# A two-layer generator block on one core: early loads for C and D, bias tables, first modulation in four column groups, first sums by token rows

## The chip, the cores and the metric

The kernel runs on one core of one Trainium2 chip. The metric is the device time of one execution in microseconds (us). A core has TensorE (PE: matrix products; PEld is its weight load), VectorE (DVE), ScalarE (ACT), GpSimd (POOL) and SyncE (SP), which here issues nearly all DMAs; sixteen DMA engines move the data. SBUF and PSUM are the core's two on-chip memories, and PSUM takes what TensorE writes.

## What is computed

There are 256 context tokens and 1024 latent tokens of width 1024, and two layers. Each layer normalises and modulates its input, multiplies it by one wide projection (3600 columns), gives slices of the result to four head groups A to D, and adds the output projection and an MLP of hidden width 4096. Group A is a gated linear recurrence, B a matrix memory; C is attention of every query to all keys, D attention to a window of 8 rows by 16 columns plus the context, with a learned bias by row and column distance (`rpb`). The modulation is a product of two vectors, silu(c) and silu(c_ctx), with `w_mod` (1024 by 6144 in each layer).

```python
def _layer(x, xc, c, c_ctx, w_mod, b_mod, g1, g2, w_in, lb, hgrn_g, mlstm_b, mlstm_g,
           qn_g, kn_g, rpb, w_out, w1, w2, rope, need_ctx):
    mod = jnp.split((jax.nn.silu(c) @ w_mod + b_mod)[:, None, :], 6, axis=-1)
    modc = jnp.split((jax.nn.silu(c_ctx) @ w_mod + b_mod)[None, None, :], 6, axis=-1)
    zl = _split_in(_modulate(_rmsnorm(x, g1), mod[0], mod[1]) @ w_in)
    zc = _split_in(_modulate(_rmsnorm(xc, g1), modc[0], modc[1]) @ w_in)
    ...
    a_c, a_l = _bidir_prefix(_hgrn2_scan, ...)
    ...
    b_c, b_l = _bidir_prefix(_mlstm_scan, ...)
    ...
    c_l = _merge(_gqa_latent(_apply_rope(ql, *rope), _apply_rope(kl, *rope), vl, kc_, vc_))
    d_l = _merge(_neighbourhood_attn(nq, nk, nv, ck, cv, rpb))
    y = jnp.concatenate([a_l, b_l, c_l, d_l], axis=-1) @ w_out
    x = x + mod[2] * y
    x = x + mod[5] * _sqrelu_mlp(_modulate(_rmsnorm(x, g2), mod[3], mod[4]), w1, w2)
    ...

def reference(...):
    for l in range(DEPTH):
        x, xc = _layer(...)
    return _rmsnorm(x, final_norm_g)
```

## The kernel before

**Tiling.** Tokens are cut into ten tiles of 128, and these into three blocks `TBS` of 256 (the context), 512 and 512. A float32 product is taken as three matmuls of two-part operands (`mm3`, L380 to L382: hi by hi, lo by hi, hi by lo). For each weight chunk a DMA brings `raw`, POOL makes the high part (L136) and DVE the low part (L145). `job` runs a projection over a list of token tiles (kind T, tokens on the partitions) or blocks (kind F, features on the partitions).

**Order.** The code is written as stages, and a scheduler reorders each engine's instructions by the program's order and its own estimate of times; an engine then runs its list in order, and SP's list of DMAs is such a list. SBUF places come from pools, and a pool opened on a place that another has left waits for the last reader of what was there.

**Stages.** `build` runs `start` for each block (x or ctx rows are loaded as `xt`, transposed on TensorE, squared by feature rows and summed), with `modulation_pe` for the chunks of 512 columns 0, 2, 1, 3 of `w_mod`, and `norm`. `modulation_pe` multiplies with two weight columns, so an accumulation of 8 matmuls fills 2 partitions of `pm`. Then `mixing(l)` runs `project_a`, in layer 0 with chunks 4 to 11 of the modulation in between (`more`; on DVE, L249, from the `mw` ring), then `a_forward`, which reads A's inputs back from DRAM (`zA`, `zL`; L731 to L739), `project_b`, `project_c` and `project_d`, the B recurrence (`b_forward`, its products at L1037, `b_backward`), and the attention. `finish` (L668) ends a head output of A or B: transposes (L683), a copy to `ofe` on ACT (L685), and a store to `oT` issued by SP (L686).

**The bias.** `bias_pad` and `bias_rows` write each bias row 64 times, padded to 127 columns, to DRAM (`rp`); `group_d` reads it back with a skewed access pattern (`braw`) and POOL multiplies by a column mask and adds another (L1232, L1233) into `BE`. `BI` is a copy of `BE` for the inner rows.

**The attention.** `attention` opens its pools, loads `KTc`, `VSc` (C's keys and values), `KTd`, `Vd` (D's), and queries `QTc`, `QTd` tile by tile, two buffers each. The order of steps is three of C, then D and C by turns. A step's scores go to the PSUM tile `S` (L1182 for C, L1265 for D); DVE takes a maximum (L1133, L1137), ACT the exponential (L1138), and TensorE transposes (L1159) and multiplies by the values (L1203, L1296). In the first four steps `S` has one buffer, since the recurrence still holds the others; later it has three.

## Time and profile before

| what | value |
|---|---|
| time, median of 3 runs | 3778.57 us (3771.67 to 3780.75) |
| the profiled execution's own time | 3784.66 us |
| its span, first to last instruction | 3782.9 us |
| TensorE, VectorE busy | 97%, 59% of the span |
| ScalarE, GpSimd busy | 29%, 31% of the span |
| mean granted TensorE clock | 0.968 of full speed |

The rows below come from a profile of one execution. A row of the timeline gives start and duration in us, the engine, the line, the operation, the tiles written and read, the shape, how many of a kind, and in brackets the engine's idle time just before, with what ended it. A row of busy times gives a stretch, its length, the busy us of PE, PEld, DVE, ACT and POOL with the number of instructions, then TensorE's granted clock, the busy share of the DMA engines and the GB/s they moved. A row of a group by line gives a count, busy us and mean ns, and behind the second bar the idle time before it; with one line asked for, it gives ns as least, median and most, and the first and last start.

### The profile page before, as it was taken

How to read it: one execution, taken by the hardware profiler on the slowest of the kernel's cores; microseconds unless marked ns; L12 is line 12 of the kernel's file. 1: busy time of each engine (PE TensorE's matmuls, PEld its weight loads, DVE VectorE, ACT ScalarE, POOL GpSimd, SP SyncE). 2: the span in 40 equal slices, each digit the busy share in tenths (PEclk: the TensorE clock that was granted, in tenths of full speed). 3: DMA queues.
4: the chain of work that ended last, by engine and by line, in shares of the span. 5: the costliest groups of instructions: out<-in, count | busy, mean ns of one | idle time of the engine just before them, and what ended most of it. 6: DMA issues, size and time to landing. Idle time of an engine off the chain costs nothing. (4 is left out here: it accounts for less than half of the span.)

```text
span 3782.9 us, 60590 instructions
## 1 busy us (share of the span) xinstructions
PE 3654.4 (97%) x22276; PEld 3080.5 (81%) x22276; DVE 2237.0 (59%) x5368; ACT 1107.9 (29%) x2847; POOL 1155.0 (31%) x1645
## 2 busy tenths in 40 slices
...
GB/s 238 232 195 98 94 89 120 210 131 94 120 39 62 70 76 78 65 81 78 61 48 95 123 146 89 101 101 195 115 78 34 124 42 50 52 45 51 50 45 65
DMA packets 374991, 366.61 MB, mean 97 GB/s; under 512 B 63334, under 2 KB 333350, under 8 KB 372902
## 3 DMA queue, kind: packets, MB, share of 16 engines
...
## 5 line engine op out<-in xcount | busy, mean ns | idle before, releaser
L380 PE MATMUL mm<-hi,whi 128*128 128x512 f32 (+1 forms) x1948 | 721.5, 371 | 4.7 <-POOL hi L136 4.7
L381 PE MATMUL mm<-lo,whi 128*128 128x512 f32 (+1 forms) x1948 | 720.9, 370 | 2.9 <-DVE lo L145 2.9
L382 PE MATMUL mm<-hi,wlo 128*128 128x512 f32 (+1 forms) x1948 | 723.1, 371 | 0.0
L136 POOL TENSOR_SCALAR whi<-raw 128x512 fp32r<-128x512 f32 x392 | 268.7, 686 | 1126.5 <-PE mm L381 840.2
L1397 DVE SCALAR_TENSOR_TENSOR x<-mm,mod,x 128x512 f32<-128x512 f32 (+1 forms) x648 | 431.6, 686 | 195.8 <-PE mm L382 192.1
L145 DVE TENSOR_TENSOR wlo<-raw,whi 128x512 fp32r<-128x512 f32 x392 | 312.2, 798 | 311.9 <-POOL whi L136 306.7
L1381 ACT ACTIVATE r<-mm 128x512 f32<-128x512 f32 (+1 forms) x162 | 89.0, 550 | 1331.3 <-PE mm L382 1331.1
L382 PE MATMUL mm<-hh,wlo 128*128 128x512 f32 (+1 forms) x1252 | 463.1, 371 | 0.0
L381 PE MATMUL mm<-hl,whi 128*128 128x512 f32 (+1 forms) x1252 | 461.2, 370 | 1.4 <-DVE hl L145 1.4
L380 PE MATMUL mm<-hh,whi 128*128 128x512 f32 (+1 forms) x1252 | 450.2, 371 | 3.5 <-POOL hh L136 3.4
L380 PE MATMUL mm<-whi,hi 128*128 128x256 f32 (+1 forms) x1496 | 432.6, 290 | 6.5 <-POOL hi L136 3.1
L381 PE MATMUL mm<-wlo,hi 128*128 128x256 f32 (+1 forms) x1496 | 429.2, 288 | 1.2 <-DVE wlo L145 1.2
L382 PE MATMUL mm<-whi,lo 128*128 128x256 f32 (+1 forms) x1496 | 425.2, 288 | 5.2 <-DVE lo L145 5.2
L380 PEld LDWEIGHTS mm<-hi,whi 128*128 128x128 f32 x1948 | 370.0, 190 | 68.8 <-POOL hi L136 5.0
L381 PEld LDWEIGHTS mm<-lo,whi 128*128 128x128 f32 x1948 | 368.6, 189 | 67.6 <-DVE lo L145 5.3
L382 PEld LDWEIGHTS mm<-hi,wlo 128*128 128x128 f32 x1948 | 368.3, 189 | 62.7 <-issue 0.5
L380 PEld LDWEIGHTS mm<-whi,hi 128*128 128x128 f32 x1496 | 287.5, 192 | 13.0 <-POOL hi L136 4.0
L382 PEld LDWEIGHTS mm<-whi,lo 128*128 128x128 f32 x1496 | 286.0, 193 | 10.1 <-DVE lo L145 6.4
L381 PEld LDWEIGHTS mm<-wlo,hi 128*128 128x128 f32 x1496 | 287.7, 192 | 5.0 <-DVE wlo L145 1.4
L145 DVE TENSOR_TENSOR hl<-r,hh 128x512 fp32r<-128x512 f32 (+1 forms) x162 | 114.7, 708 | 294.5 <-POOL hh L136 294.5
L381 PEld LDWEIGHTS mm<-hl,whi 128*128 128x128 f32 x1252 | 236.9, 189 | 45.1 <-DVE hl L145 2.2
L380 PEld LDWEIGHTS mm<-hh,whi 128*128 128x128 f32 x1252 | 235.3, 190 | 45.7 <-POOL hh L136 4.6
...
## 6 DMA issues: line engine op xcount, KB each, us to landing
raw<-in_w_mlp SPq DMA_DIRECT2D x256, 256.0 KB
raw<-in_w_in SPq DMA_DIRECT2D x112, 256.0 KB
...
```

The source lines that it names most:

```text
L136: self.nc.gpsimd.tensor_scalar(out, in_, 1.0, 0.0, op0=ALU.mult, op1=ALU.add)
L145: self.nc.vector.tensor_tensor(lo, src, hi.bitcast(F32), op=ALU.subtract)
L380: self.nc.tensor.matmul(ps, lhsT=lh, rhs=rh, start=(k == 0), stop=False)
L381: self.nc.tensor.matmul(ps, lhsT=lh, rhs=rl, start=False, stop=False)
L382: self.nc.tensor.matmul(ps, lhsT=ll, rhs=rh, start=False, stop=(k == n - 1))
L1381: nc.scalar.activation(r[:, 0:n], ps[:, 0:n], AF.Relu)
L1397: nc.vector.scalar_tensor_tensor(xk, ps[:, 0:n], self.mod[l][:, 40 + mt, v:v + 1], xk, op0=ALU.mult, op1=ALU.add)
```

## The change

1. The bias rows in DRAM go (8 DMAs from DRAM to DRAM, half of them in layer 0's MLP). In `more` of layer 0, four calls of `bias_tables` each load two column masks for 16 query columns, broadcast to 120 rows (2 layers, 4 heads, 15 row distances), multiply and add on POOL with a skewed view of the bias rows, and store a finished table `btab`. They take three buffers of the `mw` ring. `BE` is then one load for each head and half of the partitions; the two POOL passes over `braw` go.
2. The first modulation is one accumulation: two weight columns padded to 32, and output chunk g in partitions 32g to 32g+31 of one PSUM tile. Loads are 128 rows by 1024 columns, 16 of them; the result is copied once and transposed four times. The `mw` ring has 6 buffers instead of 4 there.
3. The first sums of squares are taken by ACT from the `xt` rows (Square with an accumulated output), not from the transposed x by ACT, DVE, POOL and a matmul with ones.
4. Loads of x come behind those of `w_mod`, and those of small rows behind x; ctx and the modulation have high priority. The first two jobs of `project_a` alternate by token tiles.
5. The attention's pools and first loads are opened before `b_backward`, in the places that the activations of the projections leave. `qC` in DRAM is stored by token tile, so that a row of a `QTc` load is 2 KB instead of 512 bytes. `project_d` takes its v and q jobs by turns, block by block, with both weights loaded ahead.
6. `finish` issues its store to `oT` from ACT instead of SP (36 stores).

```diff
-    def bias_rows(self, l, part):
-
-        with self.tc.issue_after(self.last_w):
-            self.nc.sync.dma_start(out=self.rps[l].rearrange("h d q c -> (h d) q c")[:, 16 * part:16 * part + 16, :],
-                                   in_=self.rpad[60 * l:60 * l + 60, :].unsqueeze(1).broadcast_to([60, 16, 127]))
...
+    def bias_tables(self, P, part):
+
+        nc, a = self.nc, self.a
+        if part == 0:
+            self.brow = self.t(P, [120, 127], tag="rs", bufs=1)
+            nc.gpsimd.memset(self.brow, 0.0)
+            nc.sync.dma_start(out=self.brow[:, 48:79], in_=a["na_rpb"].rearrange("l h d c -> (l h d) c"))
+            self.btab = self.dp.tile([120, 64, 64], F32, name="btab", tag="btab")
+        va, bg, m = [self.t(P, [128, 2, 512], tag="mw", bufs=self.mwb)[0:120].rearrange("p c (q j) -> p (c q) j", j=64) for _ in range(3)]
+        q0 = 16 * part
+        for i, z in enumerate((va, bg)):
+            nc.sync.dma_start(out=z, in_=a["k_col"][q0:q0 + 16, i * 64:i * 64 + 64].unsqueeze(0).broadcast_to([120, 16, 64]))
+        r = self.brow[:, 0:1]
+        diag = bass.AP(tensor=r.tensor, offset=r.offset + 63 - q0, ap=[r.ap[0], [-1, 16], [1, 64]])
+        nc.gpsimd.tensor_tensor(m, diag, va, op=ALU.mult)
+        nc.gpsimd.tensor_tensor(m, m, bg, op=ALU.add)
+        nc.sync.dma_start(out=self.btab[:, q0:q0 + 16, :], in_=m)
...
+        lh = self.t(mp, [128, NK, 32], tag="lhp", bufs=1)
+        nc.gpsimd.memset(lh, 0.0)
+        nc.vector.tensor_copy(lh[:, :, 0:2], self.lhC)
         rows = self.t(pm, [128, 512], tag="pm")
-        for _, _, u, src in self.raw_wide(mp)(self.a["w_mod"][l], ch):
-            for i in range(2):
-                k = u + i
-                nc.tensor.matmul(rows[0:2, :], lhsT=self.lhC[:, k, :], rhs=src[:, i, :], start=(k == 0), stop=(k == NK - 1))
-        r = self.t(mp, [2, 512], tag="mr", bufs=1)
-        nc.vector.tensor_copy(r, rows[0:2, :])
+        for k in range(NK):
+            for c in range(2):
+                t = self.t(mp, [128, 2, 512], tag="mw", bufs=self.mwb)
+                ins = nc.sync.dma_start(out=t.rearrange("p c n -> p (c n)"), in_=self.a["w_mod"][l][k * 128:(k + 1) * 128, c * 1024:c * 1024 + 1024])
+                self.last_mod = ins.ins
+                for i in range(2):
+                    g = c * 2 + i
+                    nc.tensor.matmul(rows[g * 32:g * 32 + 32, :], lhsT=lh[:, k, :], rhs=t[:, i, :], start=(k == 0), stop=(k == NK - 1))
+        r = self.t(mp, [128, 512], tag="mr", bufs=1)
+        nc.vector.tensor_copy(r, rows)
         pt = self.t(pm, [128, 512], tag="pm")
         for m in range(4):
-            nc.tensor.transpose(pt[:, m * 2:m * 2 + 2], r[:, m * 128:m * 128 + 128], self.ident[0:2, 0:2])
-        bb = self.bmod[l][:, ch * 4:ch * 4 + 4].unsqueeze(2).broadcast_to([128, 4, 2])
-        nc.vector.tensor_tensor(self.mod[l][:, ch * 4:ch * 4 + 4, :], pt[:, 0:8].rearrange("p (m v) -> p m v", v=2), bb, op=ALU.add)
+            nc.tensor.transpose(pt[:, m * 128:m * 128 + 128], r[:, m * 128:m * 128 + 128], self.ident)
...
+        if l == 0 and which == 0:
+            ps = self.t(np_, [128, 4], tag="sqs", bufs=2)
+            nc.vector.tensor_tensor(ps[:, 0:nb], self.sqt[tb][:, 0:nb, 0], self.sqt[tb][:, 0:nb, 1], op=ALU.add)
...
-        self.qC = d("qC", [128, 4, 1280])
+        self.qC = d("qC", [NT, 128, 4, 128])
...
-        self.job(l, h, "T", 768, 256, al[:6], f0, w0)
-        self.job(l, h, "T", 256, 256, al[:6], val, w1)
+        for ts in (al[:2], al[2:6]):
+            self.job(l, h, "T", 768, 256, ts, f0, w0)
+            self.job(l, h, "T", 256, 256, ts, val, w1)
...
-        self.job(l, h, "T", 3344, 256, list(range(NT)), d_v)
-        self.job(l, h, "F", 2832, 256, [1, 2] if last else [0, 1, 2], feat(self.qD, 0.125))
...
+        w = self.a["w_in"][l]
+        wv = self.wchunk(w, 0, NK, 3344, 256)
+        wq = self.wchunk(w, 0, NK, 2832, 256, sg)
+        fq = feat(self.qD, 0.125)
+        for tb, (t0, n) in enumerate(TBS):
+            self.job(l, h, "T", 3344, 256, list(range(t0 // 128, (t0 + n) // 128)), d_v, wv)
+            if tb or not last:
+                self.job(l, h, "F", 2832, 256, [tb], fq, wq)
...
-            nc.sync.dma_start(out=self.oT[tb][:, kt:kt + 2, off:off + 128], in_=s)
+            nc.scalar.dma_start(out=self.oT[tb][:, kt:kt + 2, off:off + 128], in_=s)
...
+        t0 = NCTX if last else 0
+        qt, ots = {t: self.q_load(Q, self.qC[t], "QTc") for t in (t0, t0 + 1)}, {}
...
-                    base = self.rps[l][h, 1 - par + 7 * i:8 - par + 7 * i, :, :]
-                    src = bass.AP(tensor=base.tensor, offset=base.offset + 63, ap=[[126, 64], [64 * 127, 7], [1, 64]])
-                    nc.sync.dma_start(out=raw[par * 64:par * 64 + 64, :, :], in_=src)
-                nc.gpsimd.tensor_tensor(raw, raw, col[:, 0, :].unsqueeze(1).broadcast_to([128, 7, 64]), op=ALU.mult)
-                nc.gpsimd.tensor_tensor(BE[:, h, 7 * i:7 * i + 7, :], raw, col[:, 1, :].unsqueeze(1).broadcast_to([128, 7, 64]), op=ALU.add)
...
+            for par in range(2):
+                r0 = 60 * l + 15 * h + 1 - par
+                nc.sync.dma_start(out=BE[par * 64:par * 64 + 64, h, :, :], in_=self.btab[r0:r0 + 14, :, :].rearrange("d q j -> q d j"))
...
+        pools = ExitStack()
+        D_, K_, Q_, B_, C_ = [pools.enter_context(self.pool(n, side=side)) for n in ("gd", "gkv", "gq", "gdb", "gc")]
...
+        c = self.group_c(l, K_, C_, Q_, PS)
+        d = self.group_d(l, K_, D_, PS, B_, D_BI)
...
+            self.last_x = nc.sync.dma_start(out=xt, in_=src).ins
+            for q in range(2):
+                sq = self.t(np_, [128, 512], tag="sq", bufs=2)
+                nc.scalar.activation(sq, xt[:, q * 512:q * 512 + 512], AF.Square, accum_out=self.sqt[tb][:, off // 128, q:q + 1])
...
-        for k in range(NK):
-            self.square(np_, tb, k, xs[tb][:, k, :])
...
-                    if l == 0 and i == 3:
-                        self.bias_pad(mp)
                     for ch in ([4], [5], [6, 7], [8, 9], [10, 11], [])[i]:
                         if l == 0:
                             self.modulation(0, ch, mp, True, self.raw_wide(mp), ("ma0", "ma1"), 2)
+                    if l == 0 and i < 4:
+                        self.bias_tables(mp, i)
...
+        att, close_att = self.attention(l, Y)
         close_gx()
         self.gx, close_gx = self.open(f"gy{l}", space=PSUM, side="right")
         with self.pool(f"gbb{l}", side=X) as bb:
             self.b_backward(l, bb, tail)
         close_gb()
         close_tail()
-        self.attention(l, Y)
+        att()
+        close_att()
...
-            self.rawb, self.mwb = 2, 4
+            self.rawb, self.mwb = 2, 6
...
-                    self.start(xs, ld, np_, 0)
-                    for ch in (0, 2, 1, 3):
-                        self.modulation_pe(0, ch, mp, pm)
+                    with tc.high_priority(offset=2000):
+                        self.start(xs, ld, np_, 0)
+                        self.modulation_pe(0, mp, pm)
                     h[0] = self.norm(0, 0, 0, xs[0], acts[0][0], np_)
-                    self.setup_rows()
-                    self.lower_bound(mp)
-                    self.start(xs, ld, np_, 1)
+                    with tc.issue_after(self.last_mod):
+                        self.start(xs, ld, np_, 1)
                     h[1] = self.norm(0, 0, 1, xs[1], acts[1][0], np_)
-                    self.start(xs, ld, np_, 2)
+                    with tc.issue_after(self.last_mod):
+                        self.start(xs, ld, np_, 2)
+                    with tc.issue_after(self.last_x):
+                        self.setup_rows()
+                        self.lower_bound(mp)
                     close_ld()
                     acts.append(self.open("act2", side=Y))
```

**Order of instructions, start of the program, TensorE.** `mm` at L1458 (L1476 after) are transposes of x, `pm` is the modulation, `nn<-dg` a part of the norm, and L380 (L393 after) the first projection. Before:

```order
L340 MATMUL nn_299<-dg_296,ones 128x256
L1458 MATMUL mm_389<-ident,xt_387 128x128 x4
L268 MATMUL pm_208<-mw_213,lhC 2x512 x2
L1458 MATMUL mm_514<-ident,xt_512 128x128 x4
L268 MATMUL pm_208<-mw_217,lhC 2x512 x2
L1458 MATMUL mm_562<-ident,xt_554 128x128 x4
L340 MATMUL nn_466<-dg_461,ones 128x512
L273 MATMUL pm_227<-ident,mr_225 128x2 x4
L268 MATMUL pm_233<-mw_234,lhC 2x512 x2
L380 MATMUL mm_785<-whi_738,hi_56_303 128x256
L381 MATMUL mm_785<-wlo_739,hi_56_303 128x256
```

After:

```order
L278 MATMUL pm_172<-mw_177,lhp_169 32x512 x2
L353 MATMUL nn_261<-dg_258,ones 128x256
L278 MATMUL pm_172<-mw_181,lhp_169 32x512 x2
L278 MATMUL pm_172<-mw_233,lhp_169 32x512 x2
L283 MATMUL pm_239<-ident,mr_237 128x128 x4
L1476 MATMUL mm_314<-ident,xt_308 128x128 x4
...
L1476 MATMUL mm_498<-ident,xt_492 128x128 x4
L353 MATMUL nn_391<-dg_386,ones 128x512
L1476 MATMUL mm_504<-ident,xt_492 128x128 x4
L393 MATMUL mm_729<-whi_682,hi_45_265 128x256
L394 MATMUL mm_729<-wlo_683,hi_45_265 128x256
```

All modulation matmuls now stand ahead of all transposes of latent x, and the first projection matmul stands behind all of both; before, the three were mixed.

**Order of DMAs ahead of a_forward, SP.** `z`, `v`, `Lh` and `Ll` are A's inputs, `raw` weights of the projections. Before:

```order
L216 DMA rp_2208<-rpad 60x16x127
L731 DMA z_3037<-zA_0_658 128x768
L733 DMA v_3039<-zA_0_658 128x256
L739 DMA Lh_3041<-zL_0_668 64x2x256 x2
L739 DMA Ll_3042<-zL_0_668 64x2x256 x2
L364 DMA raw_5559<-in_w_in 128x2x256
L216 DMA rp_2208<-rpad 60x16x127
L739 DMA Lh_3307<-zL_0_670 64x2x256 x2
```

After:

```order
L377 DMA raw_5330<-in_w_in 128x2x256
L490 DMA zB_0_641<-sg_2941 128x256
L377 DMA raw_5342<-in_w_in 128x2x256
L746 DMA z_3010<-zA_0_602 128x768
L748 DMA v_3012<-zA_0_602 128x256
L754 DMA Lh_3014<-zL_0_612 64x2x256 x2
L754 DMA Ll_3015<-zL_0_612 64x2x256 x2
L754 DMA Lh_3081<-zL_0_613 64x2x256 x2
```

The `rp` copies are gone from ahead of the reads of A's inputs.

**Order of instructions at the start of layer 1's attention, TensorE.** `mx`, `bx` belong to the B recurrence (L1037, or L1052 after, stands once or twice in each of its steps); `S` are scores of C. Before:

```order
L990 MATMUL mx_27910<-SB_4906_27093,qk_27751 128x130
L1068 MATMUL bx_28022<-ve_27859,Pm_28002 128x65 x4
L869 MATMUL mx_27941<-SA_4264_23688,bst_27937 128x128
L683 MATMUL mx_27945<-ident,fsq_27844 128x128 x2
L1057 MATMUL bx_28072<-MM_27089,pick_27091 128x512
L1058 MATMUL bx_28072<-ml_27085,identr 128x512
L1027 MATMUL mx_27971<-ident,qk_27965 128x128 x2
L1182 MATMUL S_29246<-KTc_29177,QTc_29238 128x512
```

After:

```order
L698 MATMUL mx_27563<-ident,fsq_27462 128x128 x2
L1042 MATMUL mx_27589<-ident,qk_27583 128x128 x2
L1052 MATMUL mx_27598<-wv_27594,kT_27592 64x130 x2
L1083 MATMUL bx_27640<-ve_27477,Pm_27620 128x65 x4
L1062 MATMUL bx_27716<-qk_27690 128x128 x2
L1005 MATMUL mx_27635<-SB_4900_27032,qk_27476 128x130
L884 MATMUL mx_27666<-SA_4258_23627,bst_27662 128x128
L1198 MATMUL S_29162<-KTc_28771,QTc_28775 128x512
L1062 MATMUL bx_27720<-qk_27690 128x128 x2
L1072 MATMUL bx_27724<-MM_27028,pick_27030 128x512
```

Before, the first scores stand ahead of the last of the five recurrence steps that are left behind the last projection matmul; after, they stand behind the second of five.

## Rows read from the trace of the kernel before

**Rows 1.** busy time of the engines, from the page

```profile
PE 3654.4 (97%) x22276; PEld 3080.5 (81%) x22276; DVE 2237.0 (59%) x5368; ACT 1107.9 (29%) x2847; POOL 1155.0 (31%) x1645
```

**Rows 2.** busy time by stretch, columns as told above: four stretches

```profile
0.00:100.00 100.00, 79.86 (x402) 48.80 (x403) 58.59 (x114) 46.97 (x88) 38.18 (x47) 0.95 0.65 229
100.00:260.00 160.00, 159.39 (x1327) 159.24 (x1325) 128.53 (x213) 32.16 (x70) 43.78 (x52) 0.98 0.73 225
700.00:820.00 120.00, 101.72 (x587) 75.41 (x586) 91.89 (x276) 61.30 (x202) 69.50 (x89) 0.80 0.71 199
2600.00:2780.00 180.00, 145.38 (x756) 106.78 (x754) 128.58 (x389) 75.99 (x247) 87.09 (x112) 0.70 0.50 148
```

**Rows 3.** TensorE's timeline at the start of the program

```profile
52.18 0.28 PE L381 MATMUL mm<-wlo,hi 128*128 128x256 f32 x1
52.30 0.28 PE L380 MATMUL mm<-whi,hi 128*128 128x256 f32 x1
58.92 8.72 PE L268 MATMUL pm<-mw,lhC 128*2 128x512 f32 x16
```

**Rows 4.** the DMA queue's timeline at the start, and a stretch of busy times

```profile
7.79 2.27 SPq L281 DMA_DIRECT2D mw<-in_w_mod  x3
39.55 16.05 SPq L281 DMA_DIRECT2D mw<-in_w_mod  x6
...
30.00:40.00 10.00, 8.72 (x52) 5.10 (x51) 5.77 (x9) 8.03 (x15) 4.80 (x5) 1.00 1.05 391
```

**Rows 5.** groups of instructions by line, 0 to 100 us

```profile
L380 PE MATMUL mm<-whi,hi 128*128 128x256 f32 x66 | 19.5, 308 | 4.1 <-POOL hi L136 2.6 <-ACT F L495 1.4
L145 DVE TENSOR_TENSOR lo<-u,hi 128x512 fp32r<-128x512 f32 x13 | 11.1, 865 | 2.4 <-POOL hi L136 2.3
```

**Rows 6.** the stop before a_forward: TensorE, DMA queue, busy times

```profile
279.79 0.55 PE L748 MATMUL mx<-Lh,sx 128*128 128x256 f32 x1 [7.44 <-DMA Lh<-zL]
...
268.44 0.96 SPq L216 DMA_DIRECT2D rp<-rpad  x1
270.57 2.57 SPq L739 DMA_DIRECT2D Lh<-zL  x2
...
272.00:280.00 8.00, 0.56 (x4) 0.37 (x4) 0.00 (x0) 0.00 (x0) 0.00 (x0) 0.84 1.06 186
```

**Rows 7.** TensorE's timeline in the attention, two column groups

```profile
803.14 0.66 PE L1203 MATMUL op<-ptc,VSc 128*64 128x128 f32 x8 [0.16 <-ACT ptc L1200]
```

**Rows 8.** instructions of the bias and of the modulation, by line

```profile
L1232 POOL TENSOR_TENSOR braw<-braw,col x16: 1126/1136/1313, 723.8 to 2731.7; 128x448 f32<-128x448 f32 x16
...
L249 DVE SCALAR_TENSOR_TENSOR ma<-mw,lhC,ma x112: 735/742/1231, 110.7 to 256.8; 128x512 f32<-128x512 f32 x112
```

**Rows 9.** layer 0's attention: TensorE, busy times

```profile
709.15 0.39 PE L382 MATMUL mm<-hi,wlo 128*128 128x512 f32 x1
730.15 0.58 PE L1182 MATMUL S<-KTc,QTc 128*128 128x256 f32 x1
750.38 0.56 PE L1182 MATMUL S<-KTc,QTc 128*128 128x256 f32 x1
...
709.00:770.00 61.00, 54.22 (x276) 41.92 (x274) 37.82 (x113) 27.17 (x96) 27.15 (x33) 0.69 0.90 262
770.00:880.00 110.00, 98.21 (x818) 73.61 (x819) 104.46 (x380) 79.08 (x250) 79.46 (x118) 0.95 0.40 110
```

**Rows 10.** layer 1's attention: TensorE, busy times

```profile
2610.74 0.39 PE L382 MATMUL mm<-hi,wlo 128*128 128x512 f32 x1
2658.78 0.78 PE L1182 MATMUL S<-KTc,QTc 128*128 128x512 f32 x1
2672.44 0.73 PE L1182 MATMUL S<-KTc,QTc 128*128 128x512 f32 x2 [2.22 <-ACT Pc L1138]
...
2610.00:2660.00 50.00, 46.83 (x204) 36.17 (x202) 30.94 (x88) 22.05 (x80) 16.98 (x21) 0.59 0.85 279
```

**Rows 11.** the head output's store, by line

```profile
L686 SPq DMA_DIRECT2D oT<-ofe x36: 359/377/1030, 648.0 to 2760.9; - x36
```

115 lines of the change are left out of this document (48 added, 67 removed).

## The prediction

> **What bounds the kernel now.** The first view to read is the page's busy time: TensorE is busy for 97% of the span, every other engine for 59% or less [rows 1]. A change can gain only where TensorE stands idle or runs at less than its full clock, so the second view is the busy time by stretch. Idle time plus busy time times the missing clock is what a stretch loses. The first 100 us lose 20.1 + 79.9 x 0.05 = 24 us; 700 to 820 us, where layer 0's attention begins, lose 18.3 + 101.7 x 0.20 = 39 us; 2600 to 2780 us, the same place in layer 1, lose 34.6 + 145.4 x 0.30 = 78 us, and there TensorE is at 0.70 of the clock [rows 2]. The change works on these three stretches and on a fourth, a stop of 7.44 us at 272 us [rows 6]. Each has its own limit, read there. Work that TensorE keeps elsewhere is left as it is, so the sum is made of four terms.
>
> **The start.** The loads of the first modulation set the pace: they begin at 7.79 us, and the last six wait in SP's list from 39.55 to 55.60 us behind x and buffers [rows 4]. Projection matmuls begin at 52 us, but stop again for the modulation, which takes 8.72 us at 58.92 us alone [rows 3]. How late the flow is can be counted. Two matmuls of 256 columns start 0.12 us apart (52.18 and 52.30) [rows 3]; up to 100 us there are 66 triples, 198 matmuls [rows 5], so 23.8 us of work: the same as a flow without gaps from 76.2 us on.
> After the change, 16 loads of 0.524 MB come first behind ctx (1.05 MB), then x (4.19 MB). The queue moves 391 GB/s when full [rows 4]: ctx is in at 10.5 us, the modulation at 32, x at 42.7. TensorE must keep up. Eight modulation matmuls take 8.72 us, 1.09 us each [rows 3]; two after one another would take 2.18 us a load, against 1.34 us of DMA. But they go to different column groups. In the attention four matmuls of 128 columns in two groups (eight records, with their weight loads) take 0.66 us [rows 7], where the same columns one after another would cost 1.09 us: so a pair costs some 2.18 x 0.66 / 1.09 = 1.32 us, and DMA stays the limit.
> The Trainium skill speaks both for and against this pairing ("TensorE: Matmul & The Clock Gate", Part 3): it gives 2.38 times for three column tiles of 512 columns, but says that a weight load overlaps a running matmul only in another row group, and column tiles share theirs. By the first the sum stays at its 70 us; by the second a pair costs up to the 2.18 us of two in turn, and the sum would be 57 us, as in rival (a). The row of the attention holds such weight loads too, and it stands with the first.
> The first projection matmul stands behind the last x transposes, at about 44 us. The context block gives 96 matmuls, 11.5 us, then the larger blocks must be normalised: 16 low parts of 0.865 us on DVE [rows 5], and a like pass before each, beside the low parts of weights. I expect 8 us of waiting there: a flow as if begun at 52 us. **Gain 76.2 - 52 = 24, of which I take 23 us.** It is 31 without that wait, and 8 if DVE's passes hold the larger blocks for twice as long and the modulation ends late too. The sums of squares that leave DVE and POOL and the squares that move to `xt` rows on ACT cost nothing more: the ACT passes run beside loads.
>
> **The stop before a_forward.** TensorE waits 7.44 us for A's inputs; SP issued a 476 KB `rp` copy at 268.44 us, just ahead of the reads at 270.57 us, and all DMA engines are then full at 186 GB/s [rows 6]. The copies are gone from that place. A read of 0.5 MB still has to land. **Gain 6 us**, from 0 (the reads wait for the stores of their own data) to 10 (the slower clock behind the stop goes too).
>
> **Layer 0's attention.** The last projection matmul is at 709.15 us, the first scores at 730.15, the second only at 750.38 us; the DMA engines are 90% busy between, with keys, values and queries [rows 9]. Those loads now stand earlier in SP's list, with C's queries in rows of 2 KB. But behind it DVE is the limit: busy for 104.5 of 110 us from 770 us on [rows 9]. What DVE has to do is unchanged, so the gain is at most its idle time before that, 61 - 37.8 = 23 us [rows 9]. **Gain 15 us**, two thirds of that cap, since the B recurrence that fills the stretch is a chain of its own; from 5 to 22.
>
> **Layer 1's attention.** From the last projection matmul (2610.74 us) to the first scores (2658.78 us) it takes 48 us, at 0.59 of the clock with the DMA engines 85% busy [rows 10]. In TensorE's list the first scores now stand behind two of the five recurrence steps left there, not behind four. At equal steps that is 2/5 of 48 = 19 us after the last projection: 29 us earlier. I take 3 off, as mixed steps slow each other. **Gain 26 us.** The upper end is DVE's idle time from 2600 to 2780 us, 180 - 128.6 = 51 us [rows 2], less 6 for what a chain never fills: 45. The lower end is 10, when scores and steps only change places.
>
> **The other edits.** Bias tables: four parts each move three times 0.49 MB in pieces of 256 bytes, 5.9 MB. The nearest row is the `rp` copy in pieces of 508 bytes: 186 GB/s at a full queue [rows 6], so 32 us of all DMA engines, between 100 and 260 us, where they are busy for 73% and 43 us are left [rows 2]. On POOL, eight passes over 1024 elements at 1.136 us for 448 [rows 8] are 21 us, beside 43.8 us of 160 [rows 2]; 32 passes, 36 us, leave the attention. I price them at 0, and keep -5 to +21 (below). The store moved to ACT: 36 issues of 0.377 us [rows 11], 14 us on an engine that is busy for 79 of 110 us in the densest part [rows 9]: 0, from a loss of 14 to a gain of 5. The v and q jobs by turns are the same matmuls in another order: 0. A new schedule moves much else a little: plus or minus 8.
>
> **Sum.** 23 + 6 + 15 + 26 = 70 us. The profiled execution took 3784.66 us, its span and 1.8 us around it; it lies 6.1 us above the median of the runs. I start half way between, at 3781.6 us: 3711.6, so **3712 us**.
>
> **Rivals.** (a) *The column groups run one after another.* Then the modulation takes 32 x 1.09 = 35 us from 12 us on, ends at 47 instead of 32, and the x transposes behind it in TensorE's list end near 57: 13 us of the start go. Against it stands [rows 7]. 3725 us.
> (b) *A modulation chunk comes late.* Each table holds three buffers of the ring from which DVE's chunks are fed: 1.5 MB at 186 GB/s is 7.9 us, and two POOL passes of 2.6 us, 13 us in each of four parts, 53 us. DVE has only 160 - 128.5 = 31.5 us idle there [rows 2], and its chunk passes alone are 112 x 0.742 = 83 us [rows 8]. TensorE takes the column sums in order and stops for a late one: 53 - 31.5 = 21 us. For it: DVE is tight. Against: the loads of a table go out while DVE still works. 3733 us.
> (c) *The attention's first steps stay as slow.* With one `S` buffer a score waits for the exponential of the one before: 2.22 us of waiting in front of one pair [rows 10]. If that chain, and not the loads, sets the stretch, 5 us of each layer stay: 23 + 6 + 5 + 5 = 39 us. 3743 us.
> (d) *The loads are not early.* They stand earlier in the list, but a place is free only when the last projection has read its activations; if they wait there, only the start and the stop gain, 29 us. 3753 us.
> (e) *The stores stop ACT.* In `finish` the store stands on ACT ahead of the next exponential, and in the first steps the next score waits for that. If a store held ACT not for its 0.377 us but until a queue place came free, each would cost TensorE that long. It turns the sum from (70 + 11) / 36 = 2.3 us a store on; at 2.6 us the kernel takes 3781.6 - 70 + 94 = 3805 us. For it: ACT then waits in order, which SP could afford. Against it: on SP the longest of the 36 took 1.03 us [rows 11].
>
> **Chances.** A measurement of this kernel tells some 0.3%, 11 us, from no change. The forecast has 0.46, (a) 0.12, (b) 0.12, (c) 0.14, (d) 0.06, (e) 0.07; 0.03 is left for several losses together, which end near no change. Faster is the sum of the forecast and (a) to (d), 0.90, less 0.01 at its edge; same 0.04; slower 0.07. The range goes from 3672 us (start 31, stop 8, layer 0 at 18, layer 1 at 45, and 8 of the schedule: 110 us) to 3756 us, just past (d).
>
> **What would show it.** At the start: modulation matmuls one per load and done near 32 us, the first projection matmul near 44, some 330 to 350 projection records more before 100 us. At a_forward: no stop over 2 us at its first product. In layer 0: second scores within 15 us of the last projection, DVE full from then on. In layer 1: first scores some 20 us behind the last projection, and the granted clock of the 180 us around above 0.75. Wrong would be: pairs of modulation matmuls over 2 us apart (a), a new wait at the column sums near 200 us (b), waits for the exponential that grow as much as the loads shrink (c), loads that start where they did (d), or exponentials that start late behind a store (e).

## The result, and the profile after

The changed kernel takes 3727.6 us (median of 4 runs, 3723.33 to 3730.74); the kernel before took 3779.66 us beside it (median of 4, 3771.67 to 3780.79). The ratio is 0.9866, with a 95% interval of 0.9853 to 0.9878: 52 us between the medians, 1.3% by the ratio. That is 16 us above the forecast time and inside the range. The profiled execution took 3723.33 us, the fastest of its four, and the one of before 3784.66 us, above all others of that kernel; so the two traces stand 61 us apart, 9 more than the medians.

The page after, busy time and TensorE's granted clock in 40 slices:

```profile
PE 3610.4 (97%) x22244; PEld 3056.5 (82%) x22244; DVE 2218.0 (60%) x5355; ACT 1105.2 (30%) x2863; POOL 1128.3 (30%) x1613
PEclk9989999999999999999999999999899999999999
```

Busy times after, with the columns as ahead of the prediction (length, PE, PEld, DVE, ACT, POOL, clock, DMA share, GB/s); the last two stretches are the places of the two attention starts, which answer to the last two rows of [rows 2]:

```profile
0.00:100.00 100.00, 75.69 (x479) 55.80 (x480) 60.26 (x123) 49.58 (x110) 31.76 (x44) 0.91 0.77 278
100.00:260.00 160.00, 152.97 (x1243) 152.16 (x1241) 128.76 (x193) 30.31 (x64) 62.83 (x59) 0.96 0.78 233
680.00:800.00 120.00, 109.27 (x726) 83.92 (x725) 92.59 (x311) 70.63 (x243) 59.50 (x84) 0.90 0.64 166
2540.00:2720.00 180.00, 156.34 (x945) 119.15 (x943) 123.97 (x404) 84.21 (x277) 71.71 (x98) 0.85 0.54 153
```

By the sum used in the prediction, layer 1's stretch of 180 us now loses 23.7 + 156.3 x 0.15 = 47 us instead of 78, and layer 0's 120 us lose 10.7 + 109.3 x 0.10 = 22 instead of 39. (The two windows begin 16 and 43 us ahead of the last projection; cut as far ahead of it as the windows of [rows 2], 9 and 11 us, they show the same idle time and clock within 1 us and 0.01.) But the first two stretches show the other side: 100 to 260 us, which were full before (159.39 us busy, [rows 2]), now hold 7 us of idle time and a lower clock. The first 100 us lose 24.3 + 75.7 x 0.09 = 31 us instead of 24, as there is less modulation work on TensorE to fill them; that the projections still begin earlier, the ledger shows.

**A ledger.** Where the time went can be counted, since every kernel here runs the same 4800 triples of projection and MLP matmuls in nearly the same order. For the n-th third matmul of a triple (L382 before, L395 after) the table gives how many us earlier it starts than in the kernel before, by the traces. The count begins at 0, so the one called the 480th is the first behind project_a's 480. All kernels of the experiments are in it. At the 640th product late has already done far more of `a_forward`, and best3d has not yet done the column sums of two modulation chunks, so these two entries compare unequal work.

| kernel | 80th (start) | 440th | 480th (first behind project_a) | 640th (project_b) | 1080th (w_out, layer 0) | 3360th (projections, layer 1) | 3760th (MLP, layer 1) |
|---|---|---|---|---|---|---|---|
| after | 12.9 | 6.5 | 2.1 | 10.1 | 23.6 | 24.7 | 61.1 |
| spill | 17.5 | -2.7 | -12.4 | -0.1 | 12.5 | 18.1 | 53.2 |
| ser | 12.0 | -5.0 | -9.1 | -3.1 | 9.8 | 15.5 | 50.6 |
| ring2 | 13.5 | -0.7 | -0.7 | 6.1 | 17.4 | 22.9 | 60.2 |
| notab | 13.3 | 12.4 | 11.7 | 15.7 | 21.7 | 25.6 | 64.6 |
| late | 14.1 | 10.5 | 9.1 | -140.8 | -56.7 | -52.4 | -16.9 |
| late2 | 13.3 | 11.9 | 0.3 | 5.6 | 7.6 | 11.3 | 51.0 |
| best2 | 17.9 | 9.6 | -4.3 | 3.4 | 17.0 | 22.6 | 49.1 |
| best3d | 14.0 | 4.8 | 6.1 | 22.5 | -42.0 | -38.6 | -5.8 |
| otsp | 13.4 | 4.6 | -0.2 | 9.7 | 26.9 | 32.6 | 70.1 |
| attl | 13.4 | 4.4 | 0.0 | 7.9 | 13.7 | 18.1 | 53.9 |
| pools | 14.2 | 4.8 | 1.1 | 9.0 | 6.0 | 12.7 | 38.2 |
| projd | 14.1 | 5.2 | 2.8 | 7.4 | 3.0 | 6.8 | 36.7 |

For the changed kernel it reads: 12.9 us at the start, 6.4 given back up to the 440th product, 3.6 gained from there to the 640th, where the stop lies (6.5 to 10.1), 13.5 in the stage with layer 0's attention, 1.1 on the way, 36.4 in layer 1's. The 2.1 at the 480th is a short dip: the last product of project_a still leads by 6.5, TensorE then waits for column sums of the modulation, and by the 520th the lead has grown to the 10.1 of the 640th. A single trace stands behind each line. The changed kernel and the last four share everything up to project_c; they agree within 1.3 us at the 80th product and within 3 us from the 440th to the 640th. Behind that the spread is larger: between the 640th and the 1080th spill, ser and ring2, whose attention is the changed kernel's, gain 11.3 to 12.9 us, but late2 2.0.

### The profile page after: what moved, and what is told of

Read it like the earlier page. It is cut to its first block, busy times and chain, and to the rows that moved or that the text cites. A ratio compares the mean times of both kernels' runs of the same rounds, so it can differ in the third digit from the quotient of the medians.

```text
span 3721.5 us, 60435 instructions
## 1 busy us (share of the span) xinstructions
PE 3610.4 (97%) x22244; PEld 3056.5 (82%) x22244; DVE 2218.0 (60%) x5355; ACT 1105.2 (30%) x2863; POOL 1128.3 (30%) x1613
## 5 line engine op out<-in xcount | busy, mean ns | idle before, releaser
L394 PE MATMUL mm<-lo,whi 128*128 128x512 f32 (+1 forms) x1928 | 711.4, 370 | 2.5 <-DVE lo L145 2.5
L395 PE MATMUL mm<-hi,wlo 128*128 128x512 f32 (+1 forms) x1928 | 713.8, 371 | 0.0
L393 PE MATMUL mm<-hi,whi 128*128 128x512 f32 (+1 forms) x1928 | 710.8, 370 | 2.7 <-POOL hi L136 2.7
L395 PE MATMUL mm<-hh,wlo 128*128 128x512 f32 (+1 forms) x1252 | 463.0, 371 | 0.0
L393 PE MATMUL mm<-hh,whi 128*128 128x512 f32 (+1 forms) x1252 | 451.0, 372 | 3.8 <-POOL hh L136 3.6
L393 PE MATMUL mm<-whi,hi 128*128 128x256 f32 (+1 forms) x1496 | 434.5, 291 | 9.8 <-POOL whi L136 2.6
L395 PE MATMUL mm<-whi,lo 128*128 128x256 f32 (+1 forms) x1496 | 430.8, 289 | 4.2 <-DVE lo L145 4.2
L393 PEld LDWEIGHTS mm<-hi,whi 128*128 128x128 f32 x1928 | 364.7, 189 | 66.5 <-POOL hi L136 3.6
L395 PEld LDWEIGHTS mm<-hi,wlo 128*128 128x128 f32 x1928 | 363.9, 189 | 61.8 <-issue 0.7
L393 PEld LDWEIGHTS mm<-whi,hi 128*128 128x128 f32 x1496 | 288.7, 193 | 15.4 <-POOL whi L136 2.9
L395 PEld LDWEIGHTS mm<-whi,lo 128*128 128x128 f32 x1496 | 289.3, 194 | 7.7 <-DVE lo L145 4.9
L393 PEld LDWEIGHTS mm<-hh,whi 128*128 128x128 f32 x1252 | 236.2, 191 | 46.0 <-POOL hh L136 4.8
```

What stands on the lines that cost most here:

```text
L393: self.nc.tensor.matmul(ps, lhsT=lh, rhs=rh, start=(k == 0), stop=False)
L394: self.nc.tensor.matmul(ps, lhsT=lh, rhs=rl, start=False, stop=False)
L395: self.nc.tensor.matmul(ps, lhsT=ll, rhs=rh, start=False, stop=(k == n - 1))
```

## The experiments

**Stores of x held back (spill).** At the start the modulation ends near 33 us as forecast, in pairs of 1.05 us, each waiting for its load. Rows of TensorE after:

```profile
30.82 1.05 PE L278 MATMUL pm<-mw,lhp 128*32 128x512 f32 x4 [0.23 <-DMA mw<-in_w_mod]
32.10 1.05 PE L278 MATMUL pm<-mw,lhp 128*32 128x512 f32 x4 [0.23 <-DMA mw<-in_w_mod]
...
48.35 0.36 PE L393 MATMUL mm<-whi,hi 128*128 128x256 f32 x1
...
58.48 0.51 PE L393 MATMUL mm<-whi,hi 128*128 128x256 f32 x2 [1.35 <-POOL whi L136]
60.29 0.39 PE L394 MATMUL mm<-wlo,hi 128*128 128x256 f32 x1 [1.31 <-DVE wlo L145]
...
67.40 0.80 PE L393 MATMUL mm<-xhi,hi 128*128 128x256 f32 x2 [2.07 <-POOL xhi L136]
```

The first projection starts at 48.35 us, 4 later than forecast, and between 57 and 70 us TensorE waits for weights, their low parts and the norm; DVE is busy for 9.5 of the 10 us from 60 to 70, and TensorE's granted clock falls to 0.58. The second row below runs from the first projection to the 80th triple:

```profile
60.00:70.00 10.00, 5.17 (x17) 3.00 (x18) 9.51 (x14) 6.16 (x11) 5.77 (x7) 0.58 0.33 121
48.35:90.47 42.12, 34.93 (x248) 32.35 (x246) 34.00 (x61) 27.13 (x54) 20.61 (x24) 0.84 0.64 229
```

SP's list shows stores of x to DRAM (`xd`) among the weight loads, and the stretch of busy times behind it the DMA engines full at 424 GB/s:

```profile
20.17 4.67 SPq L274 DMA_DIRECT2D mw<-in_w_mod  x4
24.89 7.56 SPq L1468 DMA_DIRECT2D xt<-in_x  x8
...
46.63 0.85 SPq L1573 DMA_DIRECT2D xd<-x  x2
48.20 1.72 SPq L377 DMA_DIRECT2D raw<-in_w_in  x2
51.27 0.34 SPq L1573 DMA_DIRECT2D xd<-x  x1
```

```profile
50.00:60.00 10.00, 7.64 (x63) 7.23 (x61) 8.31 (x20) 9.35 (x20) 4.92 (x5) 1.00 1.04 424
```

```diff
-                        with tc.issue_after(self.last_mod):
+                        with tc.issue_after(self.last_w):
                             nc.sync.dma_start(out=xd[i], in_=xs[i])
```

> The changed kernel with one edit: the stores of x to DRAM (xd) are held behind the last weights of the first two projection jobs instead of behind the last modulation load. Theory S (the stores fill the DMA queues from 50 to 60 us and make the weights late): the waits of TensorE between 58 and 70 us (7 us idle, 5 us lost to the clock) mostly go, the lead over the kernel before at the 80th projection product rises from 12.9 us to 17 or more. Rival D (DVE's normalisation passes are the limit there, as the prediction had it): the lead stays within 2 us of 12.9. For the whole kernel: if what is gained at the start is given back to the modulation by 262 us, the time stays at 3725 to 3730 under both; if not, S gives 3720 to 3724.

Measured: 3728.26 us (3723.44 to 3730.30), the same as the changed kernel. The lead at the 80th product rose to 17.5 us (17.9 in best2, which has this edit too), against 12.0 to 14.2 in the eleven kernels without it, so these stores do cost some 4 us of the start. But it fell to -2.7 at the 440th and -12.4 at the 480th: one store of 2 MB now lies at 110 us, among the modulation's loads, and TensorE waits for chunks and gates as it had not. SP's `xd` rows and TensorE's waits from 120 to 300 us of this run:

```profile
49.57 0.89 SPq L1573 DMA_DIRECT2D xd<-x  x2
...
109.86 0.55 SPq L1573 DMA_DIRECT2D xd<-x  x1
```

```profile
PE mm L393 <- DVE mod L260: 9.8, 2, 6.9
PE mm L393 <- DVE sg L486: 9.1, 5, 3.4
```

So the start's gain was there to be had, and the next stretch took it back and more.

**The column groups undone (ser).** Full-width weights that are zero but for two columns add all four groups in one tile.

```diff
-        lh = self.t(mp, [128, NK, 32], tag="lhp", bufs=1)
+        lh = self.t(mp, [128, NK, 224], tag="lhp", bufs=1)
...
-        nc.vector.tensor_copy(lh[:, :, 0:2], self.lhC)
+        nc.vector.tensor_copy(lh[:, :, 96:98], self.lhC)
...
-                    nc.tensor.matmul(rows[g * 32:g * 32 + 32, :], lhsT=lh[:, k, :], rhs=t[:, i, :], start=(k == 0), stop=(k == NK - 1))
+                    nc.tensor.matmul(rows, lhsT=lh[:, k, 96 - 32 * g:224 - 32 * g], rhs=t[:, i, :], start=(k == 0 and g == 0), stop=(k == NK - 1 and g == 3))
```

> The changed kernel with the first modulation's four output groups made by full-width weights (zeros but for two columns), all added in one tile, so that no two of its matmuls run side by side; loads, order and the number of matmuls are the same. The prediction's rival (a) as an edit. Pairs of matmuls should take 1.8 to 2.2 us instead of 1.05, the modulation end near 42 to 47 us instead of 33, and the lead at the 80th projection product fall from 12.9 us by 8 to 13 us. For the whole kernel: if gains at the start are given back to the modulation of the later chunks by 262 us, it loses less than 5 us, 3725 to 3733; if they are kept, 3735 to 3740.

Measured: 3732.3 us (3726.0 to 3741.53). The two kernels' modulation matmuls in the first 60 us, ser first, then after (count, busy us and mean ns, idle time before):

```profile
L278 PE MATMUL pm<-mw,lhp 128*128 128x512 f32 x64 | 28.8, 610 | 0.0
```

```profile
L278 PE MATMUL pm<-mw,lhp 128*32 128x512 f32 x64 | 16.5, 674 | 5.1 <-DMA mw<-in_w_mod 5.1
```

64 records are 32 matmuls: 0.90 us each one after another, against 16.5 / 16 = 1.03 us for a pair of two. Where two loads were there at once, the four matmuls of all four groups took 1.41 us:

```profile
10.56 1.41 PE L278 MATMUL pm<-mw,lhp 128*32 128x512 f32 x8
```

The groups run side by side, and the modulation ends 6.5 us sooner for it (33.2 against 39.7 us). Yet at the 80th product ser is only 0.9 us behind the changed kernel: its first projection starts at 50.09 us, 1.7 later. What it costs comes later: -5.0 against 6.5 at the 440th, -3.1 against 10.1 at the 640th. From 120 to 255 us TensorE waits 6.5 us for gates there, in the changed kernel 0.8; why the later start costs so much in that stretch was not taken apart. Of the whole time 5 us are left, and the two ratios' intervals overlap (0.9859 to 0.9893, 0.9853 to 0.9878).

**The bias tables left out (notab), moved (late, late2) and made smaller (ring2).** In the changed kernel the chunk passes on DVE end where they ended before, at 256.7 us ([rows 8]: 256.8), though the projections of the start are 13 us ahead. Its row, TensorE's waits from 120 to 275 us and one wait of POOL (total, times, longest):

```profile
L252 DVE SCALAR_TENSOR_TENSOR ma<-mw,lhC,ma x112: 734/742/1289, 92.7 to 256.7; 128x512 f32<-128x512 f32 x112
```

```profile
PE mm L258 <- DVE ma L252: 2.1, 2, 1.5
PE mx L763 <- DMA Lh<-zL: 2.0, 1, 2.0
```

```profile
POOL mw L218 <- DVE ma L252: 27.7, 3, 18.6
```

TensorE takes a chunk's column sums (L258) in order and waits for the passes; POOL stands for 18.6 us at once before a table, because the table's third buffer is still read by DVE. notab leaves out the making of the tables; its attention adds the column mask in the place of the bias.

```diff
-                r0 = 60 * l + 15 * h + 1 - par
-                nc.sync.dma_start(out=BE[par * 64:par * 64 + 64, h, :, :], in_=self.btab[r0:r0 + 14, :, :].rearrange("d q j -> q d j"))
+                nc.sync.dma_start(out=BE[par * 64:par * 64 + 64, h, :, :], in_=a["k_col"][0:64, 0:64].unsqueeze(1).broadcast_to([64, 14, 64]))
...
-                    if l == 0 and i < 4:
-                        self.bias_tables(mp, i)
```

> The changed kernel without the making of the bias tables: their loads, POOL passes and stores are left out, and BE is loaded from the column mask instead, in pieces of the same size. Theory T (the tables hold back the modulation's chunks): the lead at the 480th product is 8 to 12 us instead of 2.1 and at the 640th 16 to 20 instead of 10.1; 3716 to 3722 us. Rival V (the end of project_a is set by DVE's chunk passes and its DMAs with or without tables, as the run with earlier weights and the one with tables in project_b suggest, which gave back what they gained before 262 us): lead at most 5 us at the 480th product, time 3724 to 3730.

Measured: 3713.84 us (3709.06 to 3723.88), 14 us under the changed kernel. The lead stays: 12.4 at the 440th product, 11.7 at the 480th. The same chunk row and the stretch of 100 to 260 us in notab:

```profile
L252 DVE SCALAR_TENSOR_TENSOR ma<-mw,lhC,ma x112: 734/743/1231, 92.9 to 243.9; 128x512 f32<-128x512 f32 x112
```

```profile
100.00:260.00 160.00, 156.51 (x1276) 155.72 (x1274) 120.04 (x198) 32.01 (x66) 46.23 (x53) 0.96 0.66 202
```

The passes now end at 243.9 us, 13 us earlier, which is the lead of the start. DMA is at 66% instead of 78% and DVE at 120.0 us instead of 128.8. So the tables, not DVE's own passes, hold the chunks back. The five kernels with the tables and chunks of the changed kernel in project_a and its start lead by 4.4 to 6.5 us at the 440th product, the three without tables there (notab, late, late2) by 10.5 to 12.4. Against the changed kernel notab is 5.9 us ahead at the 440th, 9.6 at the 480th, in the dip, and 5.6 at the 640th. Behind layer 0's attention nothing of that is to be seen in these two traces (21.7 against 23.6 at the 1080th), and at the 3760th it is 3.5 us. Of the 14 us between the medians the ledger thus shows a small part, and the intervals of the two ratios just touch (notab 0.9818 to 0.9857, the changed kernel 0.9853 to 0.9878).

Which of their demands it is, the buffers or the rest, ring2 asked: two buffers a table instead of three.

```diff
-        va, bg, m = [self.t(P, [128, 2, 512], tag="mw", bufs=self.mwb)[0:120].rearrange("p c (q j) -> p (c q) j", j=64) for _ in range(3)]
+        va, bg, m = [self.t(P, [128, 2, 512], tag="mw", bufs=self.mwb)[0:120].rearrange("p c (q j) -> p (c q) j", j=64) for _ in range(2)] + [None]
+        m = va
```

> The changed kernel with each bias table multiplied and added in place, so that a table holds two buffers of the modulation's ring and not three; its DMAs and POOL passes are the same. Theory T by the ring: POOL no longer waits for DVE (27.7 us in the changed kernel, 18.6 us of them at once), chunks are loaded earlier, the lead at the 480th product rises by 3 us or more, time 3720 to 3725. T by the DMA queues, or rival V: less than 2 us of change, 3725 to 3730.

Measured: 3733.89 us (3724.45 to 3742.81); nothing gained, lead -0.7 at the 480th product. POOL's wait for DVE is gone, but in its place, from 100 to 265 us, it stands as long before its own passes:

```profile
POOL mw L219 <- DMA zA<-s: 18.9, 1, 18.9
POOL mw L219 <- DMA mw<-in_k_col: 13.4, 2, 9.3
```

(The second row names the table's loads; the first names a store that landed last by the profile, so what ended that wait is not sure.) The third buffer is not the cause. What is left are the two other buffers, the loads, the passes, which stand in POOL's list ahead of weight parts, and the stores; no run separates them.

Two runs moved the tables to project_b, late with buffers of 12 KB in a partition, late2 in eight small parts in two buffers of 2 KB, both in place of the calls in `more` (the calls of late2 are shown):

```diff
         self.job(l, h, "G", 1792, 272, al, bval)
+        if l == 0:
+            for i in range(4):
+                self.bias_tables(sg, i)
         self.job(l, h, "F", 1536, 256, [0, 1, 2], feat(1, 0.125))
+        if l == 0:
+            for i in range(4, 8):
+                self.bias_tables(sg, i)
```

> The changed kernel with the four bias tables built in project_b of layer 0, in buffers of their own, instead of between the modulation chunks. Theory T (the tables hold back the modulation's chunks, by its ring or by the DMA queues, and with it TensorE): the lead over the kernel before at the 480th projection product, 2.1 us in the changed kernel, rises to 8 to 12 us, and the kernel takes 3716 to 3722 us. Rival V (the chunks' own passes on DVE are the limit, so any gain at the start is given back): the lead stays at 2 to 4 us and the time at 3724 to 3730 us. If the tables in project_b disturb the projections there, up to 5 us come on top under both.

> The changed kernel with the bias tables built in project_b of layer 0, as eight small parts in place and in small buffers of their own, so that the order of project_b against a_forward stays as in the changed kernel. Theory T (the tables hold back the modulation's chunks and so TensorE): the lead over the kernel before at the 480th projection product is 8 to 12 us instead of 2.1, the lead at the 640th 16 to 20 instead of 10.1, and the kernel takes 3717 to 3722 us. Rival V (DVE's own chunk passes set the end of the modulation): lead at the 480th product at most 4 us, time 3725 to 3730 us.

Measured: late 3803.26 us (3800.01 to 3809.77), late2 3736.98 (3731.86 to 3747.19). Up to the 440th product both keep the lead (10.5 and 11.9), as the theory has it. Then each lost it in its own way. In late all of project_b came behind all of `a_forward` in TensorE's list, presumably for want of SBUF places for the larger pool, and `a_forward`'s products had nothing to fill their waits; the busy times of 300 to 400 us:

```profile
300.00:400.00 100.00, 84.54 (x536) 74.76 (x537) 67.23 (x243) 34.44 (x85) 15.84 (x14) 0.80 0.24 76
```

In late2 passes and loads of tables stand among the gates' passes and stores, and ahead of A's inputs, in the lists of POOL and SP. TensorE's waits from 200 to 330 us:

```profile
PE mm L394 <- ACT sg L485: 8.8, 3, 4.1
PE mx L770 <- DMA Lh<-zL: 5.2, 1, 5.2
```

So the expected totals were missed by 15 us and more. In late2 a cost came along with the tables to their new place (0.3 at the 480th product); in late it was the order of project_b.

**The attention: code place, SBUF places, order of project_d (attl, pools, projd).** After, TensorE goes from the last projection to the first scores in 12.5 us in layer 0 and 15.2 in layer 1; [rows 9, 10] had 21 (and 41 to the second) and 48:

```profile
695.89 0.39 PE L395 MATMUL mm<-hi,xlo 128*128 128x512 f32 x1
...
708.40 0.35 PE L1198 MATMUL S<-KTc,QTc 128*128 128x256 f32 x1 [1.42 <-DMA QTc<-qC]
709.38 0.35 PE L1198 MATMUL S<-KTc,QTc 128*128 128x256 f32 x1
```

```profile
2583.45 0.48 PE L395 MATMUL mm<-hi,xlo 128*128 128x512 f32 x1
...
2598.64 0.77 PE L1198 MATMUL S<-KTc,QTc 128*128 128x512 f32 x1
```

Before, in layer 1, SP issued C's keys at 2617 us and its queries 20 us later, with D's loads between:

```profile
2617.22 0.52 SPq L1168 DMA_DIRECT2D KTc<-kC  x1
...
2628.34 0.32 SPq L1220 DMA_DIRECT2D KTd<-kD  x1
...
2637.39 0.52 SPq L1120 DMA_DIRECT2D QTc<-qC  x1
```

After, the keys leave 42 us ahead of the last projection, and the queries 6 us behind it:

```profile
2541.74 0.42 SPq L1183 DMA_DIRECT2D KTc<-kC  x1
...
2589.20 2.46 SPq L1135 DMA_DIRECT2D QTc<-qC  x3
```

attl opens everything behind `b_backward` again; pools does that and lays the places out as before.

```diff
-        att, close_att = self.attention(l, Y)
         close_gx()
...
         close_tail()
+        att, close_att = self.attention(l, Y)
         att()
```

```diff
-        D_, K_, Q_, B_, C_ = [pools.enter_context(self.pool(n, side=side)) for n in ("gd", "gkv", "gq", "gdb", "gc")]
+        B_, C_, D_ = [pools.enter_context(self.pool(n, side=side)) for n in ("gdb", "gc", "gd")]
...
-        c = self.group_c(l, K_, C_, Q_, PS)
-        d = self.group_d(l, K_, D_, PS, B_, D_BI)
+        c = self.group_c(l, C_, C_, C_, PS)
+        d = self.group_d(l, D_, D_, PS, B_, D_BI)
```

> The changed kernel with the attention's pools and loads opened behind b_backward again, as before, and all else as changed (queries in rows of 2 KB, bias tables, the order of project_d). If the early opening is what the two attention stages gained from, layer 0 loses 12 to 17 us and layer 1 30 to 35 us: 3770 to 3780 us. If the smaller loads, the tables and the order of project_d carry a good part, it stays below 3755 us.

> The changed kernel with the attention's pools as before in two ways: opened behind b_backward (as in attl, which left both attention stages nearly as fast as in the changed kernel) and in the old order of places (gdb, gc, gd, with keys, values and queries in gc and gd). Theory P (what counts is the places: keys, values and queries lie where the activations leave early, and the scheduler then hoists the loads by itself): layer 1 loses 25 to 35 us of its 34 and layer 0 10 to 15, so 3765 to 3778 us, and the loads of KTc start at the last projection as before. Rival Q (smaller query loads, no bias work on POOL in this stretch, and the order of project_d carry the gain): less than 12 us are lost, below 3742.

Measured: attl 3727.9 us (3721.7 to 3729.32), the changed kernel's time; pools 3746.39 (3738.62 to 3749.61). SP's rows in layer 1, attl (last projection at 2590.1 us) and then pools (at 2594.8):

```profile
2548.38 0.42 SPq L1183 DMA_DIRECT2D KTc<-kC  x1
...
2595.92 2.32 SPq L1135 DMA_DIRECT2D QTc<-qC  x3
```

```profile
2593.04 0.33 SPq L1183 DMA_DIRECT2D KTc<-kC  x1
2593.88 1.11 SPq L1135 DMA_DIRECT2D QTc<-qC  x2
```

attl's keys still leave 42 us before the last projection: the scheduler lifts a load as far as its place allows, wherever the code opens it. In pools the keys wait until 2 us before the last projection, with the queries right behind. So the places let the loads go early, as the change says; the position in the code moves no load and leaves the time as it was. But the places are worth only 18.5 us of the 50 that the ledger gives the two attention stages. By the ledger (3360th to 3760th) layer 1 gains 35.8 us in attl and still 25.5 in pools; its first scores come 17.3 us behind the last projection. Layer 0 (640th to 1080th) gains 5.8 in attl and loses 3.0 in pools; the 5.8 of attl, against 13.5 after, lies in the spread of that stage told at the ledger.

It is not the early keys of C that the places are worth. In pools the first scores come 11.5 and 17.3 us behind the last projection, about as after (12.5 and 15.2), though the keys leave 40 us later. What comes late are D's loads, keys and queries; in layer 1, first the changed kernel, then pools:

```profile
2547.51 0.58 SPq L1235 DMA_DIRECT2D KTd<-kD  x1
...
2581.46 1.86 SPq L1135 DMA_DIRECT2D QTd<-qD  x3
```

```profile
2612.34 3.57 SPq L1235 DMA_DIRECT2D KTd<-kD  x4
...
2637.23 0.52 SPq L1135 DMA_DIRECT2D QTd<-qD  x1
```

Against the last projection that is 36 and 2 us ahead in the changed kernel, 18 and 42 us behind in pools. That pools loses its time by these loads is likely by this, not shown by a run of its own.

projd takes the v job for all tiles and then the q job.

```diff
-        w = self.a["w_in"][l]
-        wv = self.wchunk(w, 0, NK, 3344, 256)
-        wq = self.wchunk(w, 0, NK, 2832, 256, sg)
-        fq = feat(self.qD, 0.125)
-        for tb, (t0, n) in enumerate(TBS):
-            self.job(l, h, "T", 3344, 256, list(range(t0 // 128, (t0 + n) // 128)), d_v, wv)
-            if tb or not last:
-                self.job(l, h, "F", 2832, 256, [tb], fq, wq)
+        self.job(l, h, "T", 3344, 256, list(range(NT)), d_v)
+        self.job(l, h, "F", 2832, 256, [1, 2] if last else [0, 1, 2], feat(self.qD, 0.125))
```

> The changed kernel with project_d in its old order: the v job for all tiles, then the q job, weights loaded when each begins. Theory: the turns by block free the first activations early, without that the keys and values start later: layer 1's first scores come 5 to 15 us later against the last projection, 3732 to 3745 us in all. Rival: nothing hangs on it, as the prediction priced it (0): 3724 to 3731.

Measured: 3745.03 us (3733.8 to 3747.54), 17 us slower than the changed kernel. First scores come 25.6 us (layer 0) and 26.4 us (layer 1) behind the last projection, 13 and 11 us more than after, and layer 0's stage loses 4.4 us where the changed kernel gains 13.5. The keys of layer 1 leave only 13 us ahead of the last projection (at 2604.06 us), where the changed kernel's lead is 42:

```profile
2591.15 0.58 SPq L1177 DMA_DIRECT2D KTc<-kC  x1
```

So the turns by token block, priced at 0, are what empties the places in time. Without them layer 1 still gains 29.9 us, and with the old places 25.5; no run has both edits undone, so how far the two need each other is not shown.

What carries the 25 us that layer 1 still gains in pools was not taken apart. In pools, as in all kernels from after on, C's first queries stand directly behind its keys in SP's list (before, D's keys, values and part of the bias stood between), they come in rows of 2 KB, and POOL has no bias passes; the turns of project_d are there too. Which of the four it is stays open.

**The stores on ACT (otsp).**

```diff
-            nc.scalar.dma_start(out=self.oT[tb][:, kt:kt + 2, off:off + 128], in_=s)
+            nc.sync.dma_start(out=self.oT[tb][:, kt:kt + 2, off:off + 128], in_=s)
```

> The changed kernel with the head outputs' stores issued by SP again, as before. The prediction priced this edit at 0, from a loss of 14 to a gain of 5 us; its rival (e) had the stores stop ACT. Theory 0: 3725 to 3732 us. If the stores on ACT cost something, this run is faster than 3722; if SP's list was what they freed, slower than 3733.

Measured: 3722.91 us (3714.51 to 3725.95); ratio to the kernel before 0.9847 (0.9831 to 0.9864), beside 0.9866 (0.9853 to 0.9878) of the changed kernel: 5 us less, but the intervals overlap, so that SP is the better place is likely and not shown. What is shown is that rival (e) does not occur. In the changed kernel the 36 issues on ACT took 0.367 us each, the longest 0.422:

```profile
L701 ACTq DMA_DIRECT2D oT<-ofe x36: 366/367/422, 638.5 to 2725.7; - x36
```

**Two attempts at a faster kernel (best2, best3d).** best2 joins spill, late2 and otsp. best3d makes chunks 10 and 11 of the modulation, which only the MLP needs, in project_d, flushes deferred work behind each token block there, and has the stores on SP.

```diff
         fq = feat(self.qD, 0.125)
+        if l == 0:
+            for ch in (10, 11):
+                self.modulation(0, ch, sg, True, self.raw_narrow(sg), ("ma0", "ma1"), 2)
...
+            self.flush()
...
-                    for ch in ([4], [5], [6, 7], [8, 9], [10, 11], [])[i]:
+                    for ch in ([4], [5], [6], [7, 8], [9], [])[i]:
```

> Three edits together on the changed kernel: tables in project_b in small buffers, x stores behind the first weights, head outputs' stores issued by SP. If the tables are what gives the start's gain back, the lead kept at the 640th product is 20 to 24 us (start 17.5, plus the stop that is gone), and with 5 us of the stores the kernel takes 3707 to 3714 us. If DVE's passes set the end of the modulation, 3718 to 3724.

> The changed kernel with two chunks of the modulation, 10 and 11, which only the MLP needs, made in project_d instead of project_a, chunk 6 and 7 spread, and the head outputs' stores issued by SP. If the amount of chunk work on DVE and its loads set the end of project_a (rival V), a quarter of it gone keeps the start's lead: 9 to 13 us at the 480th product, about 20 at the 640th, and with the 5 us of the stores 3708 to 3716 us, the fastest of all. If the tables are the cause and the chunks are not, 3720 to 3726.

Measured: best2 3730.61 us (3727.24 to 3735.59), best3d 3793.76 (3788.6 to 3803.07). Of its 17.9 us best2 still had 9.6 at the 440th product and -4.3 at the 480th, where the tables stand as in late2; that they are the cause here is likely, not shown. best3d had the best lead of all at the 640th product, 22.5 us, but part of it is work that it has yet to do: column sums of two chunks, which in the changed kernel fill 253.43 to 261.15 us with their waits. And at the 440th it had 4.8, as the kernels with all chunks have. So that less chunk work frees project_a is not shown. project_d then came behind most of B's recurrence, for want of places or by the flushes, and the recurrence ran nearly alone from 560 to 700 us:

```profile
560.00:700.00 140.00, 108.59 (x589) 83.47 (x588) 89.18 (x273) 55.42 (x199) 43.09 (x54) 0.75 0.36 107
```

Neither beats the changed kernel.

## Why the prediction was right, and where its steps were off

The direction was right, the time lies in the range, and each of the four stages gained; the sum of 70 us stands against 61 us between the two traces and 52 between the medians.

- **The start: 23 forecast, 12.9 measured.** The loads, the pairs and the end of the modulation came as worked out (33 us, paced by DMA), and so did the size of the waiting, which was put at 8 us: between the first projection and the 80th triple TensorE is idle for 42.12 - 34.93 = 7.2 us. Two steps failed. The first projection was to start at 44 us and started at 48.35. And the clock behind the waits was left out: 34.93 us of work at 0.84 lose 5.6 us. Together they are about the 10 us that are missing. The x stores account for some 4 us of it by spill; their place among the weight loads had not been looked at.
- **The bias tables: 0 forecast, 5.6 us lost up to the 640th product** (9.6 in the dip at the 480th). This is a mis-sized term, though what of it is left at the end is not settled. Rival (b) had the mechanism with a price of 21 us and a chance of 0.12, against which stood that the loads go out while DVE works. The average of spare DMA time, 43 us of 160, did not tell that tables, chunks, weights and stores stand in the same lists. Of the price that (b) put on the ring's buffers one buffer was tried, and it changed nothing; the other two were not.
- **The stop: 6 forecast.** The wait fell from 7.44 to 2.0 us, and the lead grew by 3.6 us from the 440th product to the 640th, in notab by 3.3: the dip at the column sums is taken up by the wait that is left.
- **Layer 0's attention: 15 forecast, 13.5 measured; layer 1's: 26 forecast, 36.4 measured.** First scores come 15.2 us behind the last projection, where 19 were expected, and the granted clock of the 180 us went to 0.85, where over 0.75 was asked. The 19 was summed wrongly: four steps in 48 us make 24 us for two, not 19, and the gain by that reasoning 21 us, not 26. So layer 1's term is short by 15 us by its own reasoning: the first scores came sooner than the order of the steps alone would bring them. The mechanism named, loads that leave earlier, is half of it: the places are worth 18.5 us, project_d's turns, priced at 0, cost 17 us when undone, and 25 us of layer 1 stay without a cause.
- **Readings and sums.** The 66 triples up to 100 us are those of one group of operands; 71 start by then, so the flow before was 1.8 us earlier than taken. The sign of 330 to 350 projection records more before 100 us doesn't follow from the sum: 23 us at 0.12 us are 192, and 108 more came (107 triples).
- **Rivals.** (a) fell: a pair costs 1.03 us. Undone, the groups cost 0.9 us at the 80th product, 13 at the 640th and 5 in the whole time. (c) and (d) fell by the ledger, (e) by the issue row. The range held.

The start fell short by 10 us and layer 1 came out 10 over, so that the sum is as near as it is was in part luck. Behind the start stands a rule that the prediction broke: the four terms were added as if independent. The start's gain and the chunks behind it were not: spill, which moved one store from the one to the other, was 4.6 us ahead of the changed kernel at the 80th product, 14.5 behind it at the 480th and 10.2 at the 640th.
